# A diffusion backbone step: the feed-forward part's two-operand elementwise work goes from GpSimd to VectorE

## The chip, the cores and the metric

The kernel runs on one core of one Trainium2 chip. The metric is the device time of one execution in microseconds, the median over several runs. The engines are PE (TensorE, matmuls; PEld its weight loads), DVE (VectorE), ACT (ScalarE), POOL (GpSimd) and SP (which issues most DMAs). Each takes its instructions in a fixed order of its own; what waits at the head of an engine's queue holds everything behind it.

## The reference, cut to what matters

Four layers, each a token mixer (of four kinds) and a SwiGLU feed-forward part, over 640 tokens (512 latent and 128 context tokens) of 1024 features:

```python
x = x + m[2] * mixer(modulate(rms_norm(x, norm1_g), m[0], m[1])) @ w_o
h = modulate(rms_norm(x, norm2_g), m[3], m[4])
x = x + m[5] * ((silu(h @ w_gate) * (h @ w_up)) @ w_down)      # 1024 -> 2816 -> 1024
```

Everything is float32. The modulation `m` differs between latent and context tokens.

## The kernel before

**Split products.** PE gets each float32 operand as two tiles, a rounded copy (`whi`, `hh`, `ah`) made by ACT and the remainder (`wlo`, `hl`, `al`) made by a subtraction of two SBUF tiles, and does three matmuls (hi·hi, hi·lo, lo·hi) for each product. `two` (L315 to L320) makes such a pair of a 128x512 weight block; `self.sub` (L608) is the subtraction helper.

**Feed-forward part of a layer** (`rest`, L802 on). It runs in four stages, with the order of instructions on each engine set by a scheduler that follows the priorities in which the code is written.

1. The second half of the mixer's output projection (`halves_first`): 8 feature blocks `d`, each 24 matmuls, then DVE adds the result into `x` (L603), ACT squares (L494, tile `t`), DVE sums the squares (L496). POOL (L621) or ACT (L623) scales `x` by a column for the norm (`scaled`).
2. `make_b` builds the right operands of a one-level Strassen-Winograd product out of the normed activations: DVE multiplies by `rstd` (L656), sums and differences (`T1` to `T4`) follow, and each is split by its inner `two` (hi on ACT at L645 or L648, lo at L608 or L649).
3. Eleven pairs of `gate_up` units (`gate` and `up` for `i` = 0 to 10). A unit loads four 128x512 weight blocks (tiles `raw`), `make_a` forms the sums `S1` to `S4` (L696, tiles `sum`), and seven calls of `block` each split one block and issue 12 matmuls of 128x320 into three PSUM banks `a`, `b`, `d` (tile name `big`). Between them DVE reads the banks (L722, into `sv` or `y`). The accumulation goes on in a bank only when DVE has read it. An `up` unit ends with three products `y*v` (L735), two casts `ah` (L760, ACT) and two subtractions `al` (L608).
4. After pairs 3, 6, 9 and 11 the down projection of the pairs done so far. In the first three layers pieces of the next layer's modulation (`rawm`, `mod`) are filled in.

The four `raw` slots are reused in turn, so the next unit's weight loads wait for the last reader of the old block.

Of the kernel before, what the change touches and what calls it, by code (L numbers as in the profile page):

```python
# [8 lines left out]
F32 = mybir.dt.float32  # L9
F32R = mybir.dt.float32r  # L10
AF = mybir.ActivationFunctionType
ALU = mybir.AluOpType
# [4 lines left out]
ND = 8  # L17
# [19 lines left out]
HALF = ND // 2  # L37
# [225 lines left out]
class Net:  # L263
# [51 lines left out]
    def two(self, raw, eng):  # L315

        hi, lo = (self.slot(n)[:, :raw.shape[1]] for n in ("whi", "wlo"))
        self.nc.scalar.copy(hi, raw)  # L318
        eng.tensor_tensor(lo, raw, hi.bitcast(F32), ALU.subtract)  # L319
        return hi, lo  # L320
# [304 lines left out]
    def make_b(self, pool, L, B, raws):  # L625

        nc = self.nc
        lo, hi = slice(0, 320), slice(320, T)  # L630
        t3 = [pool.tile([P, 2, 320], F32, tag="a", name="raw", bufs=12) for _ in range(HALF // 2)]
        slots = [self.new_act() for _ in range(ND)]
        for tag, w in (("c", T), ("d", 320)):
            slots += [[pool.tile([P, w], F32R, tag=x + tag, name=x, bufs=HALF) for x in ("hh", "hl")] for _ in range(HALF)]
        shift = self.mods[L][0][:, 24:24 + ND]
        more = pool.tile([P, ND + HALF], F32, tag="more", name="more")
        self.sub(nc.gpsimd, more[:, :ND], shift[:, :, 1], shift[:, :, 0])
        self.sub(nc.gpsimd, more[:, ND:], shift[:, HALF:, 0], shift[:, :HALF, 0])

        done = []  # L640

        def two(name, slot, c, x, bias=None, eng=nc.vector):
            h, l = (y[:, c] for y in slots[slot])
            if bias is None:
                nc.scalar.copy(h, x)  # L645
                done.append(self.sub(eng, l, x, h.bitcast(F32)))
            else:
                nc.scalar.activation(h, x, AF.Identity, bias=bias)  # L648
                done.append(eng.scalar_tensor_tensor(l, x, bias, h.bitcast(F32), ALU.add, ALU.subtract))  # L649
            B.setdefault(name, []).append((h, l))  # L650

        def raw(d, c):
            with contextlib.ExitStack() as st:
                if len(done) >= 2:
                    st.enter_context(self.tc.issue_after(done[-2].ins))
                nc.vector.tensor_tensor(raws[d][:, c], raws[d][:, c], self.rstd[:, c], ALU.mult)  # L656

        for d in range(ND):
            raw(d, lo)
            two(("11", "21")[d // HALF], d, lo, raws[d][:, lo], shift[:, d, 0:1])  # L660
            yield
        for i in range(HALF):
            for d in (i, i + HALF):
                raw(d, hi)
                p, m = raws[d][:, NL:], more[:, d:d + 1]
                nc.scalar.activation(p, p, AF.Identity, bias=m)
            a, b, t = raws[i], raws[i + HALF], t3[i // 2][:, i % 2]
            self.sub(nc.vector, t, b[:, hi], a[:, hi])
            self.sub(nc.gpsimd, a[:, hi], a[:, hi], a[:, lo])
            two("T1", i, hi, a[:, hi])  # L670
        for i in range(HALF):
            a, b, t = raws[i], raws[i + HALF], t3[i // 2][:, i % 2]
            nc.vector.tensor_tensor(a[:, lo], t, a[:, lo], ALU.add)
            two("T2", ND + i, lo, a[:, lo], shift[:, i + HALF, 0:1])
            self.sub(nc.gpsimd, b[:, lo], b[:, lo], a[:, lo])
        for i in range(HALF):
            two("T3", ND + i, hi, t3[i // 2][:, i % 2], more[:, ND + i:ND + i + 1])
        for i in range(HALF):
            two("T4", ND + HALF + i, lo, raws[i + HALF][:, lo], eng=nc.gpsimd)
        for i in range(HALF):  # L680
            two("22", i + HALF, hi, raws[i + HALF][:, hi], shift[:, i + HALF, 0:1])
        yield

    def make_a(self, L, name, i):

        nc = self.nc
        at = [WIDX[L, name, f][0] for f in (i, i + NF // 2)]
        raw = {}
        for n in ("21", "22", "11", "12"):
            raw[n] = self.slot("raw")  # L690
            nc.sync.dma_start(raw[n], self.a["wall"][at[int(n[0]) - 1] + int(n[1]) - 1])
        for n, x, y, op in (("S1", "21", "22", ALU.add), ("S2", "S1", "11", ALU.subtract),
                            ("S3", "11", "21", ALU.subtract), ("S4", "12", "S2", ALU.subtract)):
            raw[n] = self.slot("sum")
            eng = nc.vector if n in ("S1", "S2") else nc.gpsimd
            eng.tensor_tensor(raw[n], raw[x], raw[y], op)  # L696
        return raw

    def block(self, out, A, B, start, stop, eng=None):

        h, l = self.two(A, eng or self.nc.vector)
        for k, (xh, xl) in enumerate(B):
            c = slice(k * P, (k + 1) * P)
            self.mm(out, h[:, c], xh, start and k == 0, False)
            self.mm(out, h[:, c], xl, False, False)
            self.mm(out, l[:, c], xh, False, stop and k == len(B) - 1)

    def gate_up(self, fp, L, name, i, B, pair):

        nc = self.nc  # L710
        up = name == "up"
        A = self.make_a(L, name, i)

        eng = nc.vector if i else nc.gpsimd
        a, b, d = (self.ps("big")[:, :320] for _ in range(3))
        t = fp.tile([P, 3, 320], F32, tag="sv", name="sv", bufs=2)
        s1, v1, v2 = (t[:, m] for m in range(3))
        if not up:
            pair.extend(fp.tile([P, T], F32, tag="t", name="y", bufs=4) for _ in range(2))

        def add(out, x, y):
            nc.vector.tensor_tensor(out, x, y, ALU.add)  # L722

        def result(r, c, src, v=None):

            y = pair[r][:, 320 * c:320 * c + 320]
            if not up:
                if v is not None:
                    add(y, src, v)
                self.silu = nc.scalar.activation(y, src if v is None else y, AF.Silu)  # L730
            elif v is None:
                nc.vector.tensor_tensor(y, y, src, ALU.mult)
            else:
                add(v, src, v)
                nc.gpsimd.tensor_tensor(y, y, v, ALU.mult)  # L735

        self.block(a, A["11"], B["11"], True, True, eng)
        yield
        nc.scalar.copy(s1, a)
        self.block(a, A["12"], B["21"], False, True, eng)  # L740
        result(0, 0, a)
        yield
        if i == 0:
            self.block(d, A["S1"], B["T1"], True, True, eng)
        self.block(b, A["S2"], B["T2"], True, True, eng)
        add(v1, b, s1)
        if i:
            self.block(d, A["S1"], B["T1"], True, True, eng)
        self.block(b, A["S3"], B["T3"], False, True)
        yield  # L750
        add(v2, b, s1)
        result(1, 1, d, v2)
        self.block(b, A["22"], B["T4"], False, True)
        result(1, 0, b, s1)
        self.block(d, A["S4"], B["22"], False, True)
        result(0, 1, d, v1)
        if up:
            for r in (1, 0):
                hi, lo = (fp.tile([P, T], F32R, tag="a", name=n, bufs=12) for n in ("ah", "al"))
                nc.scalar.copy(hi, pair[r])  # L760
                self.sub(nc.gpsimd, lo, pair[r], hi.bitcast(F32))
                pair[r] = (hi, lo)
        yield

# [993 lines left out]
```

## Time and profile before

| | |
|---|---|
| median of 3 runs | 3245.66 us (3241.69 to 3249.45) |
| the profiled execution | 3248.49 us, its span 3246.7 us |
| busy in the span | PE 3043.1 us (94%), DVE 2170.4 (67%), ACT 1527.9 (47%), POOL 1257.4 (39%) |
| feed-forward parts | four, some 500 us each |

The span runs from the first to the last instruction. Busy time counts an instruction from its start to its end, waiting for a port included.

### The profile page before, as it was taken

How to read it: one execution, taken by the hardware profiler on the slowest of the kernel's cores; microseconds unless marked ns; L12 is line 12 of the kernel's file. 1: busy time of each engine (PE TensorE's matmuls, PEld its weight loads, DVE VectorE, ACT ScalarE, POOL GpSimd, SP SyncE). 2: the span in 40 equal slices, each digit the busy share in tenths (PEclk: the TensorE clock that was granted, in tenths of full speed). 3: DMA queues.
4: the chain of work that ended last, by engine and by line, in shares of the span. 5: the costliest groups of instructions: out<-in, count | busy, mean ns of one | idle time of the engine just before them, and what ended most of it. 6: DMA issues, size and time to landing. Idle time of an engine off the chain costs nothing. (4 is left out here: it accounts for less than half of the span.)

```text
span 3246.7 us, 58033 instructions
## 1 busy us (share of the span) xinstructions
PE 3043.1 (94%) x21901; PEld 2845.8 (88%) x21901; DVE 2170.4 (67%) x4166; ACT 1527.9 (47%) x3296; POOL 1257.4 (39%) x1175
## 2 busy tenths in 40 slices
PE   8998889999989989999987898999999989799999
PEld 6997879999988779999975677899998878799999
DVE  5555486766576768667668766866765775867665
ACT  4455453433356654334346665433434575534332
POOL 2453362322244454323235445432322553633322
PEclk9998999999999999999998999999999999899999
DMA  7346552233433342222311224422433111122222
GB/s 264 94 122 206 174 196 87 80 106 104 143 104 128 110 153 74 80 82 82 88 46 39 62 74 150 145 77 82 133 106 120 43 37 43 40 85 83 77 85 78
DMA packets 163640, 331.46 MB, mean 102 GB/s; under 512 B 19104, under 2 KB 49184, under 8 KB 163360
## 3 DMA queue, kind: packets, MB, share of 16 engines
q1 hardware_dynamic: 160192, 323.47, 32.3%
q8 instruction: 173, 2.83, 0.4%
q10 hardware_dynamic: 3168, 4.28, 0.4%
q14 instruction: 107, 0.88, 0.1%
HBM read 303.86 MB, written 4.28 MB: 95 GB/s over the span
## 5 line engine op out<-in xcount | busy, mean ns | idle before, releaser
L271 PE MATMUL big<-hh,whi 128*128 128x320 f32 x2720 | 829.5, 314 | 31.3 <-ACT hh L645 12.0
L271 PE MATMUL big<-hl,whi 128*128 128x320 f32 x2720 | 832.9, 312 | 9.6 <-DVE hl L649 5.3
L271 PE MATMUL big<-hh,wlo 128*128 128x320 f32 x2720 | 823.6, 311 | 0.0
L318 ACT CAST whi<-raw 128x512 fp32r<-128x512 f32 (+3 forms) x668 | 388.5, 587 | 655.3 <-PE big L271 407.7
L319 DVE TENSOR_TENSOR wlo<-raw,whi 128x512 fp32r<-128x512 f32 (+1 forms) x504 | 439.2, 874 | 207.0 <-ACT whi L318 204.6
L271 PEld LDWEIGHTS big<-hh,whi 128*128 128x128 f32 x2720 | 509.8, 190 | 47.0 <-DVE sv L722 16.7
L271 PEld LDWEIGHTS big<-hl,whi 128*128 128x128 f32 x2720 | 511.3, 189 | 19.7 <-DVE hl L649 10.6
L271 PEld LDWEIGHTS big<-hh,wlo 128*128 128x128 f32 x2720 | 509.3, 189 | 0.4
L319 DVE TENSOR_TENSOR wlo<-sum,whi 128x512 fp32r<-128x512 f32 x336 | 304.6, 911 | 75.3 <-ACT whi L318 72.5
L319 POOL TENSOR_TENSOR wlo<-raw,whi 128x512 fp32r<-128x512 f32 (+2 forms) x164 | 225.2, 1385 | 305.4 <-ACT whi L318 274.1
L318 ACT CAST whi<-sum 128x512 fp32r<-128x512 f32 x352 | 216.0, 617 | 267.7 <-PE big L271 222.2
L271 PE MATMUL big<-al,whi 128*128 128x320 f32 x1408 | 334.0, 310 | 3.2 <-POOL al L608 3.2
L271 PE MATMUL big<-ah,whi 128*128 128x320 f32 x1408 | 332.0, 311 | 1.2 <-ACT ah L760 1.2
L271 PE MATMUL big<-ah,wlo 128*128 128x320 f32 x1408 | 333.1, 310 | 0.0
L1044 POOL TENSOR_SCALAR p<-p,st 128x640 f32<-128x640 f32 (+2 forms) x256 | 199.4, 784 | 297.0 <-DVE st L1043 188.1
L696 POOL TENSOR_TENSOR sum<-raw 128x512 f32<-128x512 f32 x88 | 124.8, 1418 | 410.3 <-DMA raw<-in_wall 242.3
L735 POOL TENSOR_TENSOR y<-y,sv 128x320 f32<-128x320 f32 x132 | 146.4, 1116 | 346.1 <-DVE sv L722 321.6
L696 POOL TENSOR_TENSOR sum<-raw,sum 128x512 f32<-128x512 f32 x88 | 121.3, 1379 | 404.2 <-ACT whi L318 161.9
L603 DVE SCALAR_TENSOR_TENSOR x<-big,mod,x 128x320 f32<-128x320 f32 (+2 forms) x480 | 182.3, 432 | 107.7 <-PE big L271 107.7
L271 PEld LDWEIGHTS big<-al,whi 128*128 128x128 f32 x1408 | 239.6, 189 | 4.1 <-POOL al L608 3.7
L271 PEld LDWEIGHTS big<-ah,whi 128*128 128x128 f32 x1408 | 238.0, 188 | 4.7 <-issue 2.5
L271 PEld LDWEIGHTS big<-ah,wlo 128*128 128x128 f32 x1408 | 239.3, 189 | 0.2
(264 smaller groups left out, 6093.7 us busy)
## 6 DMA issues: line engine op xcount, KB each, us to landing
raw<-in_wall SPq DMA_DIRECT2D x644, 256.0 KB, 2.6
rawm<-in_wmod SPq DMA_DIRECT2D x176, 512.0 KB, 5.9
k<-k SPq DMA_DIRECT2D x38, 384.0 KB, 4.5
raw<-in_wall SPq DMA_DIRECT2D x96, 128.0 KB, 2.1
bias<-in_nabias SPq DMA_DIRECT2D x16, 576.0 KB, 7.2
raw<-in_wmod SPq DMA_DIRECT2D x32, 256.0 KB, 5.8
qpe<-pes SPq DMA_DIRECT2D x56, 80.0 KB, 2.1
out_y<-x ACTq DMA_DIRECT2D x8, 320.0 KB, 2.2
```

The costliest lines, as they stand in the source:

```text
L271: return self.nc.tensor.matmul(out, lhsT=lhsT, rhs=rhs, start=start, stop=stop, skip_group_check=True)
L318: self.nc.scalar.copy(hi, raw)
L319: eng.tensor_tensor(lo, raw, hi.bitcast(F32), ALU.subtract)
L603: self.last = self.nc.vector.scalar_tensor_tensor(xs, halves[b][:, p0:p1], self.mcol(L, i, d, c), xs, ALU.mult, ALU.add)
L696: eng.tensor_tensor(raw[n], raw[x], raw[y], op)
L735: nc.gpsimd.tensor_tensor(y, y, v, ALU.mult)
L1044: nc.gpsimd.tensor_scalar(p, p, rd, 1.0, ALU.mult, ALU.mult)
```

## The change

Every elementwise instruction with two tensor operands in the feed-forward part that stood on POOL is issued to DVE. In each layer these are 44 sums `S3` and `S4` (128x512), 8 `wlo` of the two units with `i` = 0, 33 products `y*v` (128x320), 22 `al` (128x640), and in `make_b` 12 of 128x320 and two tiny ones: 121 instructions, 484 in all. POOL keeps the scaling at L621, 12 instructions in each layer, and all it does in the mixers.

```diff
@@ make_b
-        self.sub(nc.gpsimd, more[:, :ND], shift[:, :, 1], shift[:, :, 0])
-        self.sub(nc.gpsimd, more[:, ND:], shift[:, HALF:, 0], shift[:, :HALF, 0])
+        self.sub(nc.vector, more[:, :ND], shift[:, :, 1], shift[:, :, 0])
+        self.sub(nc.vector, more[:, ND:], shift[:, HALF:, 0], shift[:, :HALF, 0])
...
-            self.sub(nc.gpsimd, a[:, hi], a[:, hi], a[:, lo])
+            self.sub(nc.vector, a[:, hi], a[:, hi], a[:, lo])
             two("T1", i, hi, a[:, hi])
...
             two("T2", ND + i, lo, a[:, lo], shift[:, i + HALF, 0:1])
-            self.sub(nc.gpsimd, b[:, lo], b[:, lo], a[:, lo])
+            self.sub(nc.vector, b[:, lo], b[:, lo], a[:, lo])
...
-            two("T4", ND + HALF + i, lo, raws[i + HALF][:, lo], eng=nc.gpsimd)
+            two("T4", ND + HALF + i, lo, raws[i + HALF][:, lo])
@@ make_a
             raw[n] = self.slot("sum")
-            eng = nc.vector if n in ("S1", "S2") else nc.gpsimd
-            eng.tensor_tensor(raw[n], raw[x], raw[y], op)
+            nc.vector.tensor_tensor(raw[n], raw[x], raw[y], op)
@@ block and gate_up
-        h, l = self.two(A, eng or self.nc.vector)
+        h, l = self.two(A, self.nc.vector)
...
-        eng = nc.vector if i else nc.gpsimd
...
-                nc.gpsimd.tensor_tensor(y, y, v, ALU.mult)
+                nc.vector.tensor_tensor(y, y, v, ALU.mult)
...
-                self.sub(nc.gpsimd, lo, pair[r], hi.bitcast(F32))
+                self.sub(nc.vector, lo, pair[r], hi.bitcast(F32))
```

The scheduler writes the orders anew. Three places follow. The changed file is three lines shorter, so that L695, L719, L727 and L732 of it are L696, L722, L730 and L735 of before.

The first is DVE in stage 1 of layer 0, from the first sum of the first `gate_up` unit on. Before:

```order
L696 TENSOR_TENSOR sum<-raw 128x512
L603 SCALAR_TENSOR_TENSOR x<-big,mod,x 128x320
L603 SCALAR_TENSOR_TENSOR x<-big,mod,x 128x192
L603 SCALAR_TENSOR_TENSOR x<-big,mod,x 128x128
L696 TENSOR_TENSOR sum<-sum,raw 128x512
L603 SCALAR_TENSOR_TENSOR x<-big,mod,x 128x320
L603 SCALAR_TENSOR_TENSOR x<-big,mod,x 128x192
L603 SCALAR_TENSOR_TENSOR x<-big,mod,x 128x128
L496 TENSOR_TENSOR t<-t 128x640
```

And now:

```order
L695 TENSOR_TENSOR sum<-raw 128x512
L603 SCALAR_TENSOR_TENSOR x<-big,mod,x 128x320
L603 SCALAR_TENSOR_TENSOR x<-big,mod,x 128x192
L603 SCALAR_TENSOR_TENSOR x<-big,mod,x 128x128
L695 TENSOR_TENSOR sum<-raw 128x512
L695 TENSOR_TENSOR sum<-sum,raw 128x512
L319 TENSOR_TENSOR wlo<-raw,whi 128x512
L695 TENSOR_TENSOR sum<-raw,sum 128x512
L603 SCALAR_TENSOR_TENSOR x<-big,mod,x 128x320
L603 SCALAR_TENSOR_TENSOR x<-big,mod,x 128x192
L603 SCALAR_TENSOR_TENSOR x<-big,mod,x 128x128
L319 TENSOR_TENSOR wlo<-raw,whi 128x512
```

`S3`, `S4` and the first `wlo` now stand ahead of the residual additions of `d` = 1; `S4` and the `wlo` need weight blocks that DMAs bring.

The second is ACT in stage 2 of layer 0, around its change of function table; `hh<-raw` at L645 is the first `T1` copy, on which PE waits. Before:

```order
L648 ACTIVATE hh<-raw,more 128x320
L648 ACTIVATE hh<-raw,mod 128x320
L318 CAST whi<-sum 128x512
L730 ACT_TABLE_LOAD
L730 ACTIVATE y<-big 128x320
L645 CAST hh<-raw 128x320
```

And now:

```order
L318 CAST whi<-sum 128x512
L727 ACT_TABLE_LOAD
L727 ACTIVATE y<-big 128x320
L648 ACTIVATE hh<-raw,more 128x320
L648 ACTIVATE hh<-raw,mod 128x320
L318 CAST whi<-raw 128x512
L645 CAST hh<-raw 128x320
```

Two `T` copies and one cast of weights have moved between the table load and the `T1` copy. Layers 1 and 2 show the same; in layer 3 one copy has moved.

The third is DVE at the end of an `up` unit of layer 3; the last `sv` row reads the bank of the unit after it. Before:

```order
L722 TENSOR_TENSOR sv<-big,sv 128x320
L319 TENSOR_TENSOR wlo<-raw,whi 128x512
L722 TENSOR_TENSOR sv<-big,sv 128x320
L319 TENSOR_TENSOR wlo<-sum,whi 128x512 x2
L319 TENSOR_TENSOR wlo<-raw,whi 128x512
L722 TENSOR_TENSOR sv<-big,sv 128x320
```

And now:

```order
L719 TENSOR_TENSOR sv<-big,sv 128x320
L319 TENSOR_TENSOR wlo<-raw,whi 128x512
L695 TENSOR_TENSOR sum<-raw,sum 128x512
L732 TENSOR_TENSOR y<-y,sv 128x320
L719 TENSOR_TENSOR sv<-big,sv 128x320
L319 TENSOR_TENSOR wlo<-sum,whi 128x512
L732 TENSOR_TENSOR y<-y,sv 128x320
L608 TENSOR_TENSOR al<-y,ah 128x640
L319 TENSOR_TENSOR wlo<-sum,whi 128x512
L608 TENSOR_TENSOR al<-y,ah 128x640
L319 TENSOR_TENSOR wlo<-raw,whi 128x512
L719 TENSOR_TENSOR sv<-big,sv 128x320
```

Between the same two reads of PSUM there now stand a sum, two products and two `al` more, and each `al` needs the cast `ah` from ACT. Outside the feed-forward parts the orders are the same but for a few swaps of neighbours in layer 1.

## Rows read from the trace of the kernel before

**Rows 1.** Busy time by engine, the four feed-forward parts together (384:893, 1159:1656, 1975:2482, 2748:3247).

```profile
sum 2012.00, PE 1941.55 PEld 1878.62 DVE 1367.73 ACT 797.77 POOL 724.02; mean PE 485.39 PEld 469.65 DVE 341.93 ACT 199.44 POOL 181.01
```

**Rows 2.** Chain that ended last, layer 3: start us, us, what.

```profile
2873.50 113.62 PE big L271 x773
```

**Rows 3.** Waits of PE, whole span: us in total, times, longest.

```profile
PE big L271 <- ACT hh L645: 12.0, 4, 4.0
PE big L271 <- DVE sv L722: 11.6, 16, 2.1
PE big L271 <- DVE t L496: 10.7, 9, 4.5
...
PE big L271 <- ACT hh L648: 6.7, 8, 1.7
PE big L271 <- DVE hl L649: 5.3, 8, 2.2
...
PE big L271 <- POOL al L608: 3.2, 2, 2.1
```

**Rows 4.** Three groups of DVE by line, whole span: ns min/median/max.

```profile
L319 DVE TENSOR_TENSOR wlo<-sum,whi x336: 672/686/2077, 411.7 to 3197.2; 128x512 fp32r<-128x512 f32 x168
L722 DVE TENSOR_TENSOR sv<-big,sv x308: 472/483/493, 458.3 to 3214.4; 128x320 f32<-128x320 f32 x154
L649 DVE SCALAR_TENSOR_TENSOR hl<-raw,mod,hh x64: 534/540/1424, 422.7 to 2822.9; 128x320 fp32r<-128x320 f32 x64
```

**Rows 5.** Timeline of DVE and POOL at 3192 us: start us, us.

```profile
3192.84 2.08 DVE L319 TENSOR_TENSOR wlo<-sum,whi 128x512 fp32r<-128x512 f32 x1 [0.77 <-ACT whi L318]
...
3192.78 3.57 POOL L608 TENSOR_TENSOR al<-y,ah 128x640 fp32r<-128x640 f32 x2
```

**Rows 6.** Groups by form in 2928:2999 (stage 3, layer 3): busy us, mean ns.

```profile
L319 DVE TENSOR_TENSOR wlo<-raw,whi 128x512 fp32r<-128x512 f32 x17 | 19.8, 1163 | 3.1 <-ACT whi L318 3.0
L319 DVE TENSOR_TENSOR wlo<-sum,whi 128x512 fp32r<-128x512 f32 x21 | 18.9, 899 | 3.9 <-ACT whi L318 3.8
...
L608 POOL TENSOR_TENSOR al<-y,ah 128x640 fp32r<-128x640 f32 x4 | 7.6, 1910 | 0.0
L735 POOL TENSOR_TENSOR y<-y,sv 128x320 f32<-128x320 f32 x6 | 7.4, 1242 | 6.1 <-DVE sv L722 6.1
L696 POOL TENSOR_TENSOR sum<-raw,sum 128x512 f32<-128x512 f32 x5 | 6.5, 1296 | 30.5 <-ACT whi L318 12.5 <-issue 9.1 <-DVE sum L696 8.9
L696 POOL TENSOR_TENSOR sum<-raw 128x512 f32<-128x512 f32 x4 | 5.4, 1346 | 5.3 <-DMA raw<-in_wall 3.0 <-DVE wlo L319 2.3
```

**Rows 7.** Timeline of DVE, stage 1, layer 0.

```profile
398.76 0.82 DVE L496 TENSOR_TENSOR t<-t 128x640 f32<-128x640 f32 x1 [0.81 <-ACT t L494]
399.50 1.13 DVE L603 SCALAR_TENSOR_TENSOR x<-big,mod,x 128x320 f32<-128x320 f32 x3
```

**Rows 8.** Groups by form in 420:457.2 (stage 2, layer 0): busy us, mean ns.

```profile
L649 DVE SCALAR_TENSOR_TENSOR hl<-raw,mod,hh 128x320 fp32r<-128x320 f32 x16 | 11.4, 714 | 0.4 <-ACT hh L648 0.4
L656 DVE TENSOR_TENSOR raw<-raw,rstd 128x320 f32<-128x320 f32 x16 | 10.5, 675 | 0.0
L649 DVE SCALAR_TENSOR_TENSOR hl<-raw,more,hh 128x320 fp32r<-128x320 f32 x4 | 4.7, 1172 | 0.0
...
L608 POOL TENSOR_TENSOR raw<-raw 128x320 f32<-128x320 f32 x8 | 9.6, 1213 | 7.5 <-DVE raw L608 5.9 <-DVE raw L673 1.3 <-DVE mod L439 0.4
L608 POOL TENSOR_TENSOR hl<-raw,hh 128x320 fp32r<-128x320 f32 x4 | 4.0, 1001 | 1.2 <-ACT hh L645 1.2
...
L319 POOL TENSOR_TENSOR wlo<-sum,whi 128x512 fp32r<-128x512 f32 x2 | 2.7, 1343 | 1.6 <-ACT whi L318 1.6
```

**Rows 9.** Timeline of ACT, stage 2, layer 0.

```profile
440.01 0.45 ACT L645 CAST hh<-raw 128x320 fp32r<-128x320 f32 x1
440.36 0.62 ACT L318 CAST whi<-raw 128x512 fp32r<-128x512 f32 x1
440.88 0.56 ACT L648 ACTIVATE hh<-raw,mod 128x320 fp32r<-128x320 f32 x1
```

More of the change, by code (lines that the diff above doesn't have):

```diff
@@ L636, in make_b, with two @@
         more = pool.tile([P, ND + HALF], F32, tag="more", name="more")
-        self.sub(nc.gpsimd, more[:, :ND], shift[:, :, 1], shift[:, :, 0])
-        self.sub(nc.gpsimd, more[:, ND:], shift[:, HALF:, 0], shift[:, :HALF, 0])
+        self.sub(nc.vector, more[:, :ND], shift[:, :, 1], shift[:, :, 0])
+        self.sub(nc.vector, more[:, ND:], shift[:, HALF:, 0], shift[:, :HALF, 0])
         done = []
-        def two(name, slot, c, x, bias=None, eng=nc.vector):
+        def two(name, slot, c, x, bias=None):
             h, l = (y[:, c] for y in slots[slot])
@@ L645, in two @@
                 nc.scalar.copy(h, x)
-                done.append(self.sub(eng, l, x, h.bitcast(F32)))
+                done.append(self.sub(nc.vector, l, x, h.bitcast(F32)))
             else:
                 nc.scalar.activation(h, x, AF.Identity, bias=bias)
-                done.append(eng.scalar_tensor_tensor(l, x, bias, h.bitcast(F32), ALU.add, ALU.subtract))
+                done.append(nc.vector.scalar_tensor_tensor(l, x, bias, h.bitcast(F32), ALU.add, ALU.subtract))
             B.setdefault(name, []).append((h, l))
@@ L694, in make_a, with block @@
             raw[n] = self.slot("sum")
-            eng = nc.vector if n in ("S1", "S2") else nc.gpsimd
-            eng.tensor_tensor(raw[n], raw[x], raw[y], op)
-        return raw
-    def block(self, out, A, B, start, stop, eng=None):
-        h, l = self.two(A, eng or self.nc.vector)
+            nc.vector.tensor_tensor(raw[n], raw[x], raw[y], op)
+        return raw
+    def block(self, out, A, B, start, stop):
+        h, l = self.two(A, self.nc.vector)
         for k, (xh, xl) in enumerate(B):
@@ L734, in result @@
                 add(v, src, v)
-                nc.gpsimd.tensor_tensor(y, y, v, ALU.mult)
-        self.block(a, A["11"], B["11"], True, True, eng)
+                nc.vector.tensor_tensor(y, y, v, ALU.mult)
+        self.block(a, A["11"], B["11"], True, True)
         yield
         nc.scalar.copy(s1, a)
-        self.block(a, A["12"], B["21"], False, True, eng)
+        self.block(a, A["12"], B["21"], False, True)
         result(0, 0, a)
@@ L743, in gate_up @@
         if i == 0:
-            self.block(d, A["S1"], B["T1"], True, True, eng)
-        self.block(b, A["S2"], B["T2"], True, True, eng)
+            self.block(d, A["S1"], B["T1"], True, True)
+        self.block(b, A["S2"], B["T2"], True, True)
         add(v1, b, s1)
         if i:
-            self.block(d, A["S1"], B["T1"], True, True, eng)
+            self.block(d, A["S1"], B["T1"], True, True)
         self.block(b, A["S3"], B["T3"], False, True)
```

## The prediction

> **What bounds the kernel now.** I read the busy time by engine in the feed-forward parts first, since the change is only there. PE works in 1941.55 of 2012 us [rows 1]: 70 us of idle time in four parts is all that the change can give back. Then the chain that ended last: for stretches of a hundred microseconds it is nothing but matmuls, 773 of them in 113.62 us, 0.147 us each [rows 2]. In stage 3 PE is the bound, and DVE matters only where PE waits for it. So the third view is the list of PE's waits [rows 3]. The ones that belong to the feed-forward part and that the change can reach are the first `T1` copy (L645, 12.0 us in 4 waits, one in each layer), the reads of PSUM by DVE (L722, 11.6 us in 16), the sum of squares (L496, 10.7 us in 9), the other copies and remainders of `make_b` (L648 6.7 us, L649 5.3 us), and `al` on POOL (3.2 us in 2, at the very end of a part). The fourth view is how long DVE's instructions take. The 336 `wlo` of a sum have a median of 686 ns and a longest of 2077, while the 308 reads of PSUM, of which one operand lies in SBUF, stay within 472 to 493 [rows 4]. The timeline shows what the long ones have in common: the 2.08 us `wlo` lies beside two `al` on POOL, 3.57 us together [rows 5]. DVE instructions with two operands in SBUF are held up while POOL works on SBUF too.
>
> **The change, part by part: DVE's load.** On DVE a 128x640 instruction takes 0.82 us and the next one starts 0.74 us after it [rows 7]: 0.08 us of each overlaps. A moved 128x512 then costs 0.60 us of DVE's queue (0.686 less 0.08), a 128x320 0.40 (from 0.48), an `al` 0.74.
>
> In 71 us of stage 3 [rows 6] POOL has 4 `al`, 6 products and 9 sums; on DVE they are 4 x 0.74 + 6 x 0.40 + 9 x 0.60 = 10.8 us. Against that the 17 and 21 `wlo` have means of 1163 and 899 ns where 686 is the undisturbed median: 17 x 0.477 + 21 x 0.213 = 12.6 us that end when POOL is silent. DVE's load falls by 1.8 us in place of rising. The other stretches of stage 3 repeat the pattern.
>
> The 12.6 us can be held against a rule. The Trainium skill, SBUF — State Buffer, section "SBUF: two separate sides", says that DVE with two SBUF inputs and a GpSimd instruction that reads SBUF exclude each other: whichever starts first has the shared ports for its whole length, and the other is blocked. By that rule alone up to all of POOL's work in the stretch could be put on DVE's account, and the load would fall by more; the measured means decide, and they say 12.6.
>
> In stage 2 of layer 0 [rows 8] DVE has a stretch of 37 us from the first `rstd` product to the last remainder with no idle time to speak of. Of it 16 x (0.714 - 0.540) + 16 x (0.675 - 0.48) + 4 x (1.172 - 0.540) = 8.4 us are such waits (the undisturbed times are in [rows 4]), and smaller groups of the same kind add some 3. What moves in are 8 + 4 instructions of 128x320 (4.8 us), two `wlo`, and three sums that the same view lists (5 x 0.60 = 3.0). Net 8.4 + 3 - 7.8: DVE gets through stage 2 about 4 us sooner, at least 0.6 if the small groups give nothing.
>
> **What reaches PE.** Term by term, over the four layers:
>
> - `al` at the end of a part [rows 3]: 1.9 us on POOL [rows 6] becomes 0.82 on DVE, twice in a row, and the product ahead of it 0.48 for 1.24. The wait of 3.2 us goes: -3. The bounds are -3.2 and 0, if the DVE queue holds something else by then.
> - Remainders in stage 2 (L649, 5.3 us): DVE is 4 us sooner at the end of a stretch in which these waits are 1 or 2 us long. I take -4 (bounds -5.3 and 0).
> - The `T1` copy: ACT now does two copies and a cast ahead of it [rows 9]. Start to start the cast is 0.52 us and a copy of 0.56 about 0.46, so the copy comes 1.45 us later in three layers and 0.46 in the fourth: +4.8, and PE stands still there already, so nothing hides it. The bounds are +4.8 and 0, if ACT gets to its table load sooner.
> - Copies at L648 (6.7 us in 8): some of the waits come right behind the `T1` one, for exactly the copies that now stand ahead of it. -3 (bounds -6.7 and 0).
> - Reads of PSUM (L722, 11.6 us in 16): DVE is late for them when a held-up instruction of up to 2.08 us is in front. The longest in front is now 0.82, but there are more of them. -3, bounds -9 and what the second rival says.
> - Stage 1 (L496, 10.7 us): sums and `wlo` now stand ahead of the residual additions, ten instructions or 6 us in some 25 us, where DVE has idle time like the 0.81 us in front of its row [rows 7]. Moving the `raw` blocks' readers to DVE frees the slots sooner, too, while S4 waiting for its DMA holds the additions. I take 0, bounds -6 and +6.
> - The two tiny subtractions, and `wlo` of the first units, are in the loads above; weight DMAs are issued by SP as before, and the slots come free at about the same time.
>
> The sum is -3 - 4 + 4.8 - 3 - 3 + 0 = -8.2 us against the profiled execution's 3248.49, so 3240.3. The median of the runs shown is 2.8 us under that execution; for a median I say 3237.
>
> **The rivals.**
>
> *Hidden.* PE bounds the kernel, and each microsecond won in stage 2 is lost at the `T1` copy or in stage 1. For it: the gains in the list are no larger than the doubtful terms. Against it: three of the five waits have their cause removed. Time: the terms -3 and -4 against +4.8, with the rest at zero, -2: 3243.
>
> *DVE in front of PSUM (slower).* In a `gate_up` unit the bank `b` goes on accumulating only when DVE has read it, and what covers that read is one block of 12 matmuls, 12 x 0.147 = 1.76 us [rows 2]. At the end of an `up` unit a sum, two products and two `al` now stand between two reads, 0.60 + 0.80 + 1.48 = 2.9 us of work, and an `al` waits for a cast on ACT. If the read comes 1 us later than its cover in each of the 44 `up` units, it costs 44 us: 3290. It decides as soon as the mean delay beyond the cover exceeds 8.2/44 = 0.19 us. Against it: in the 71 us of [rows 6] DVE's load does not rise, and over the whole span PE waited for these reads 16 times only [rows 3]. By the Trainium skill, Perfetto Trace Analysis, section "Optimizing Scalar/DVE Operations", a saturated DVE is a reason to put work on Scalar or even GPSIMD, which speaks against this change; the same section warns that between those two it might not help, as they share a read port. DVE at 1367.73 of 2012 us [rows 1], waits included, isn't saturated over a part, but it is in stage 2.
>
> *More comes back.* If stage 1 gives its 6 us and the reads their 9 as well, with -3, -5 and -6 from the others and the `T1` copy no later: about -29, so 3217.
>
> *The change doesn't do what it says.* The 48 scalings stay on POOL and go on colliding with DVE in stage 1. That leaves stage 1 as it is, which the 0 for it already says.
>
> **How the numbers follow.** The forecast of about -8 has a chance of 0.50 and by itself runs from -16 to -4; hidden 0.27; slower 0.16; more 0.07. The range of 3221 to 3256 reaches from most of the large gain to a mean delay beyond the cover of (3256 - 3237)/44 = 0.43 us in front of PSUM, and leaves out the rest of both, under 0.2. A difference of 0.2%, 6.5 us, is about what a measurement of this kernel can tell from none. Of the forecast 0.43 lies beyond it, and all of the large gain: faster 0.50. Hidden and the small end of the forecast are the same: 0.33. Slower 0.17.
>
> **What would show it.** Right: `wlo` of a sum with a longest time under 1 us in stage 3; DVE's busy time over the span within 2% of before though it has 484 instructions more; PE's wait for `al` gone, for L649 under 2 us; its wait for L645 up to some 16 us. Wrong: PE's waits for the reads of PSUM grown to 20 us and more (the second rival), waits for L496 or for the residual additions grown (stage 1), or DVE busy far above 2170 us, which would say that the long `wlo` had another cause than POOL.

## The result, and the profile after

The changed kernel takes 3219.73 us (median of 4 runs, 3214.83 to 3222.39) against 3247.55 us before (4 runs): a ratio of 0.9913, 95% interval 0.9891 to 0.9935. That is 27.8 us less, where 8.2 were forecast. The direction is right, the size is a third of what came, and 3219.73 lies just under the range (3221 to 3256); the rival *more comes back* had said 3217.

The forecast of DVE's load held. In the feed-forward parts (windows view; busy us by engine, the four parts summed) DVE is busy 1397.67 us for 1367.73 [rows 1], though 484 instructions more stand on it:

```profile
sum 1984.70, PE 1924.07 PEld 1870.83 DVE 1397.67 ACT 804.62 POOL 82.75; mean PE 481.02 PEld 467.71 DVE 349.42 ACT 201.15 POOL 20.69
```

In the 71 us of stage 3 of [rows 6], DVE was busy 56.91 us with 83 instructions. The same place of the changed kernel (windows view: stretch, then busy us and instructions of PE, PEld, DVE, ACT and POOL, granted clock):

```profile
2907.00:2978.00 71.00, 71.00 (x486) 71.00 (x485) 54.08 (x101) 32.67 (x61) 0.00 (x0) 1.00 0.28 84
```

101 instructions in 54.08 us: DVE does more and is busy for less, since the long instructions are gone. The three groups of [rows 4], after (ns min/median/max):

```profile
L319 DVE TENSOR_TENSOR wlo<-sum,whi x352: 673/684/694, 397.0 to 3164.8; 128x512 fp32r<-128x512 f32 x176
L719 DVE TENSOR_TENSOR sv<-big,sv x308: 475/484/493, 448.0 to 3183.6; 128x320 f32<-128x320 f32 x154
L649 DVE SCALAR_TENSOR_TENSOR hl<-raw,mod,hh x64: 533/543/554, 415.6 to 2795.7; 128x320 fp32r<-128x320 f32 x64
```

The longest `wlo` of a sum falls from 2077 to 694 ns, the longest `hl` from 1424 to 554; the reads of PSUM were never long and are the same.

PE's waits over the span, after (us in total, times, longest; they answer to [rows 3]):

```profile
PE sm L271 <- DMA rawm<-in_wmod: 30.0, 13, 4.8
...
PE big L271 <- DVE t L496: 8.3, 6, 3.5
...
PE big L271 <- ACT hh L645: 5.2, 2, 4.4
...
PE big L271 <- DVE hl L649: 3.4, 8, 1.1
...
PE big L271 <- DVE sv L719: 2.2, 2, 1.6
...
PE big L271 <- ACT hh L648: 1.7, 2, 1.2
...
PE big L271 <- DVE al L608: 0.3, 1, 0.3
```

Every wait that the prediction priced got smaller, and one that it didn't name got larger. The same view of before had, for the modulation's blocks:

```profile
PE sm L271 <- DMA rawm<-in_wmod: 9.0, 5, 2.4
```

So the sum of the list says less than it seems to. A better account is PE's *lost time*, worked out from the records of all matmuls: from each start to the next, less the pace of its form at full clock (0.147 us for 128x320; 2.05 us is set for the 32 matmuls of a modulation piece, where an undisturbed one in stage 3 adds 1.96, so the account is 0.1 us too low for each piece, before and after alike). A low granted clock is in it, the useful work of a piece is not. An entry is good to some 1 us where a piece stands at the border of two columns. In us, layers 0 to 3:

| | stage 1 | stage 2 and the first two units | the rest of the part | sum |
|---|---|---|---|---|
| before | 5.1, 3.6, 3.5, 11.1 | 12.9, 16.3, 13.2, 20.9 | 8.2, 11.9, 7.6, 6.0 | 120.3 |
| after | 5.9, 3.3, 3.3, 9.4 | 13.5, 14.4, 17.8, 15.8 | 3.8, 5.4, 3.8, -0.7 | 95.7 |

The feed-forward parts give back 24.6 us, and 21.4 of these lie behind the first two units: in stage 3, where PE waited for the reads of PSUM, and at the ends of the parts. Counted from start to start, the reads alone are 12.1 us of it (13 of the 16 waits of before lie there, and none after), `al` and `ah` some 4, and a low granted clock some 3. Stage 2 gives 5.1 us in layer 3, and in layers 0 to 2 it loses 3.3. The profiled executions differ by 33.7 us (3248.49 to 3214.83); what is left lies in the mixers, where orders hardly changed. PE starts stage 1 of layer 0 at 384.5 us before and 375.7 after; in the runs below, whose first mixer has the same code, it starts between 376.4 and 385.2. So some 9 us between two single profiles can be chance, and times are compared by medians.

Where PE waited for a read. Before, in the last `up` unit ahead of the first down projection of layer 0 (timeline of DVE, then of POOL: start us, us):

```profile
505.33 2.07 DVE L319 TENSOR_TENSOR wlo<-sum,whi 128x512 fp32r<-128x512 f32 x1 [0.77 <-ACT whi L318]
507.32 2.05 DVE L319 TENSOR_TENSOR wlo<-raw,whi 128x512 fp32r<-128x512 f32 x1
509.29 0.48 DVE L722 TENSOR_TENSOR sv<-big,sv 128x320 f32<-128x320 f32 x1
...
502.68 2.63 POOL L735 TENSOR_TENSOR y<-y,sv 128x320 f32<-128x320 f32 x2
505.27 3.55 POOL L608 TENSOR_TENSOR al<-y,ah 128x640 fp32r<-128x640 f32 x2
```

Both `wlo` ahead of the read at 509.29 lie beside the two `al` on POOL: 3.96 us from the start of the first to the read. After, at the same place, both `al` are on DVE as well:

```profile
496.57 0.81 DVE L608 TENSOR_TENSOR al<-y,ah 128x640 fp32r<-128x640 f32 x1
497.31 0.68 DVE L319 TENSOR_TENSOR wlo<-sum,whi 128x512 fp32r<-128x512 f32 x1
497.91 0.81 DVE L608 TENSOR_TENSOR al<-y,ah 128x640 fp32r<-128x640 f32 x1
498.65 0.68 DVE L319 TENSOR_TENSOR wlo<-raw,whi 128x512 fp32r<-128x512 f32 x1
499.25 0.48 DVE L719 TENSOR_TENSOR sv<-big,sv 128x320 f32<-128x320 f32 x1
```

Four instructions in 2.68 us where two took 3.96. Such a wait, 0.2 to 1.3 us long, stood ahead of 10 of the 12 down projections that end the first three groups of pairs; after, there is none.

### The profile page after: what moved, and what is told of

It reads as the page before. It is cut to its first block, busy times and chain, and to the rows that moved or that the text cites. A ratio compares the mean times of both kernels' runs of the same rounds, so it can differ in the third digit from the quotient of the medians.

```text
span 3213.0 us, 57617 instructions
## 1 busy us (share of the span) xinstructions
PE 3027.1 (94%) x21901; PEld 2839.4 (88%) x21901; DVE 2199.0 (68%) x4650; ACT 1534.5 (48%) x3296; POOL 606.8 (19%) x691
## 5 line engine op out<-in xcount | busy, mean ns | idle before, releaser
L271 PEld LDWEIGHTS big<-hl,whi 128*128 128x128 f32 x2720 | 510.0, 189 | 11.9 <-DVE hl L649 6.5
L319 POOL TENSOR_TENSOR wlo<-raw,whi 128x512 fp32r<-128x512 f32 (+2 forms) x148 | 197.0, 1343 | 1638.2 <-ACT whi L318 1600.5
L319 DVE TENSOR_TENSOR wlo<-raw,whi 128x512 fp32r<-128x512 f32 (+1 forms) x520 | 329.6, 638 | 119.2 <-ACT whi L318 116.0
L271 PE MATMUL big<-al,whi 128*128 128x320 f32 x1408 | 327.4, 309 | 0.3 <-DVE al L608 0.3
L271 PE MATMUL big<-ah,whi 128*128 128x320 f32 x1408 | 325.4, 310 | 0.4 <-ACT ah L757 0.3
L319 DVE TENSOR_TENSOR wlo<-sum,whi 128x512 fp32r<-128x512 f32 x352 | 241.0, 685 | 60.2 <-ACT whi L318 57.8
L271 PE MATMUL sm<-whi,hh 128*128 128x256 f32 (+1 forms) x770 | 224.2, 296 | 2.1 <-DVE qs L287 1.2
L271 PE MATMUL sm<-wlo,hh 128*128 128x256 f32 (+1 forms) x770 | 222.6, 291 | 0.2 <-POOL wlo L319 0.2
L271 PE MATMUL sm<-whi,hl 128*128 128x256 f32 (+1 forms) x770 | 222.7, 291 | 0.0
```

The lines of the kernel that those rows point to most:

```text
L271: return self.nc.tensor.matmul(out, lhsT=lhsT, rhs=rhs, start=start, stop=stop, skip_group_check=True)
```

## The experiments

The times are medians, and each ratio is to runs of the kernel before that were taken beside that run. The lost times are of one profiled execution each. Five runs move a part of the change, and tail_back moves the rest of it:

| moved to DVE | label | us | ratio to before (95%) | PE's lost time: stage 1, 2, rest |
|---|---|---|---|---|
| all (the change) | | 3219.73 | 0.9913 (0.9891 to 0.9935) | 21.9, 61.5, 12.3 |
| products and `al` | tail_only | 3217.23 | 0.9915 (0.9902 to 0.9928) | 25.2, 60.4, 13.4 |
| `al` | al_only | 3228.83 | 0.9947 (0.9930 to 0.9964) | 25.7, 65.6, 17.6 |
| products | products_only | 3247.21 | 0.9997 (0.9986 to 1.0008) | 27.0, 61.6, 35.5 |
| sums `S3`, `S4` | sums_only | 3244.30 | 0.9995 (0.9986 to 1.0004) | 34.4, 60.6, 20.6 |
| `make_b`, first `wlo` | stage2_only | 3248.86 | 1.0009 (1.0000 to 1.0018) | 19.3, 55.9, 36.3 |
| all but products and `al` | tail_back | 3229.72 | 0.9951 (0.9939 to 0.9964) | 25.6, 58.3, 19.3 |
| nothing | before | 3246.31 to 3248.55 | | 23.3, 63.3, 33.7 |

**tail_only.** Against before:

```diff
-                nc.gpsimd.tensor_tensor(y, y, v, ALU.mult)
+                nc.vector.tensor_tensor(y, y, v, ALU.mult)
...
-                self.sub(nc.gpsimd, lo, pair[r], hi.bitcast(F32))
+                self.sub(nc.vector, lo, pair[r], hi.bitcast(F32))
```

> Only the products y*v and the al remainders go to DVE; the sums S3 and S4, the first wlo and all of make_b stay on POOL. Theory A (POOL's products and al lengthen the DVE instructions that stand in front of a read of PSUM, and PE then waits for that read): PE's wait for sv falls from 11.6 us to about 3, the wait for al from 3.2 to under 0.5, and the time is 12 to 15 us under before, about 3234. Rival B (DVE's load: the sums still collide, and DVE has 55 instructions of a layer more): the waits for sv stay at 10 or grow, and the time is within 5 us of before.

55 of a layer's 121 instructions give the whole gain; the run cannot be told from the full change. The waits for `sv` fall from 11.6 us to

```profile
PE big L271 <- DVE sv L720: 2.6, 5, 0.8
```

Theory A's waits hold (no wait for `al` is left), its time does not: it expected 12 to 15 us, and 29 came. Rival B falls: the sums go on colliding, and tail_only is no slower than the full change for it.

**sums_only.** Against before:

```diff
-            eng = nc.vector if n in ("S1", "S2") else nc.gpsimd
-            eng.tensor_tensor(raw[n], raw[x], raw[y], op)
+            nc.vector.tensor_tensor(raw[n], raw[x], raw[y], op)
```

> Only the sums S3 and S4 go to DVE. Theory A: the waits for sv in front of the down projections stay (8 to 12 us), since the products and al still run on POOL at that place, and so do the waits for al; the time is 0 to 5 us under before. Rival C (the sums are what matters, as they are the most instructions and also free the weight slots sooner): sv under 4 us and the time 12 us under before or more.

No change in time, as theory A said, but not for its reason. In the profiled execution, the slowest of its 11, the sums do relieve stage 3 (33.7 to 20.6 us lost), and give it back in stage 1 (23.3 to 34.4): the sums that now stand ahead of the residual additions there hold up the sum of squares. About half of these 11 us are longer waits; with them the granted clock was at its lower level, 1.2 GHz, for 24 us of stage 1 in place of 3.

```profile
PE big L271 <- DVE t L496: 16.8, 7, 5.4
...
PE big L271 <- DVE sv L720: 6.3, 5, 3.0
```

**stage2_only.** Against before, the edits in `make_b` and in `block` of the change alone:

```diff
-            self.sub(nc.gpsimd, a[:, hi], a[:, hi], a[:, lo])
+            self.sub(nc.vector, a[:, hi], a[:, hi], a[:, lo])
...
-        h, l = self.two(A, eng or self.nc.vector)
+        h, l = self.two(A, self.nc.vector)
```

> Only the work of make_b and the wlo of the first two units go to DVE. Theory A: stage 2 of layers 0 to 2 gains nothing, since PE then waits for the modulation's weight blocks (rawm) in place of the T1 copy, and layer 3, which has no such pieces, gains about 5 us; the time is 4 to 6 us under before. Rival D (the 20 us of rawm waits are chance of one execution): all four layers gain 3 to 5 us each, 15 us in all.

No gain by the median. Layer 3 loses 15.4 us in stage 2 for 20.9, as in the full change, and layers 0 to 2 40.5 for 42.4. The profiled execution was the fastest of 12 (3234.11 us) and its feed-forward parts lose 8.8 us less than before, so profile and median do not agree here; what made the others slower is not known.

**tail_back.** Against the changed kernel:

```diff
-                nc.vector.tensor_tensor(y, y, v, ALU.mult)
+                nc.gpsimd.tensor_tensor(y, y, v, ALU.mult)
...
-                self.sub(nc.vector, lo, pair[r], hi.bitcast(F32))
+                self.sub(nc.gpsimd, lo, pair[r], hi.bitcast(F32))
```

> The changed kernel, with the products y*v and the al remainders back on POOL. Theory A: the waits for sv and al return with some 8 and 3 us and the time is 10 to 15 us over the changed kernel, about 3232. Rival C or D (sums or stage 2 carry the gain): within 4 us of the changed kernel, about 3221.

The time is as theory A said, 10 us over the change, and one half of its reason is wrong: `al` comes back as a wait, `sv` does not.

```profile
PE big L271 <- POOL al L608: 3.2, 2, 2.1
...
PE big L271 <- DVE sv L719: 2.2, 2, 1.5
```

With the sums off POOL its queue is short; at the place shown above the products and the first `al` start earlier, and only one `al` is left beside the `wlo` ahead of the read. So either half of the change takes away most of the waits for reads, and their gains don't add up. What only the tail gives is the ends of the parts (the rest falls from 19.3 to 12.3 us, most of the 10 us).

**al_only and products_only.** Against before, the second or the first line of tail_only's diff alone.

> Of the whole change only the 22 al remainders of a layer go to DVE; sums, products, the first wlo and make_b stay on POOL. Theory G (the two al of an up unit, 3.6 us in a row on POOL, are what lengthens the two wlo in front of the next read of PSUM, and what PE waits for at the end of a part): the time is that of the run with products and al, 3216 to 3224, with waits for sv under 4 us. Rival H (each set of collisions adds its part, and the products are half of them): half the gain, about 3232, with 5 to 8 us for sv.

> Of the whole change only the 33 products of a layer go to DVE; al, sums, the first wlo and make_b stay on POOL. Theory G (al is the main cause): al on POOL goes on lengthening the wlo in front of the reads, so sv stays at 6 to 10 us and al at 3; the time is 5 to 12 us under before, about 3238. Rival N (the products, which hold up POOL's queue and with it the casts and al behind them, are the main cause): sv under 3 us, 15 us under before or more.

`al` alone gives 18 us, between the two theories, with 6.9 us left for `sv` in 7 waits. None of the 7 stands ahead of a down projection any more: all lie in stage 2 or within 11 us behind the first two units, so theory G is right on that place and not on the whole. Products alone give nothing, where theory G expected 5 to 12 us (`sv` 14.7 us in 20), but with `al` already on DVE they give another 10 to 12. Which waits these are worth is not shown: the lost time falls by 5 us in stage 2 and by 4 behind it.

**al_decoy.** Is it the collision, or the shorter way from `ah` to PE? Against al_only, one instruction more, whose result nobody reads:

```diff
                 self.sub(nc.vector, lo, pair[r], hi.bitcast(F32))
+                self.sub(nc.gpsimd, fp.tile([P, T], F32, tag="junk", name="junk"), pair[r], hi.bitcast(F32))
```

> As the run with al alone on DVE, and beside it POOL subtracts the same two SBUF tiles once more into a tile that nobody reads; the orders on PE and DVE stay the same but for a few swaps. No result waits for POOL's copy. Theory A (the collision on SBUF makes DVE late): the wlo beside it reach 2 us again, the waits for sv come back with 6 to 10 us, and the time is 8 to 15 us over the run with al alone. Rival I (latency: PE and ACT gained since an al takes 0.82 us on DVE and 1.8 on POOL, and the place of al in the order is what counts): no wait comes back, and the time is within 3 us of the run with al alone.

3289.90 us against 3228.83: 61 us longer, ratio to before 1.0135 (1.0115 to 1.0156), four times the upper end of what theory A expected. At one place of al_only (DVE), where a sum on POOL lies beside the first `wlo` and nothing beside the rest:

```profile
594.16 1.78 DVE L319 TENSOR_TENSOR wlo<-sum,whi 128x512 fp32r<-128x512 f32 x1
595.87 0.81 DVE L608 TENSOR_TENSOR al<-y,ah 128x640 fp32r<-128x640 f32 x1
596.60 0.68 DVE L319 TENSOR_TENSOR wlo<-raw,whi 128x512 fp32r<-128x512 f32 x1
597.21 0.48 DVE L720 TENSOR_TENSOR sv<-big,sv 128x320 f32<-128x320 f32 x1
```

The same four in al_decoy (DVE, then POOL):

```profile
597.27 1.79 DVE L319 TENSOR_TENSOR wlo<-sum,whi 128x512 fp32r<-128x512 f32 x1
598.98 2.19 DVE L608 TENSOR_TENSOR al<-y,ah 128x640 fp32r<-128x640 f32 x1
601.09 2.03 DVE L319 TENSOR_TENSOR wlo<-raw,whi 128x512 fp32r<-128x512 f32 x1
603.04 0.48 DVE L720 TENSOR_TENSOR sv<-big,sv 128x320 f32<-128x320 f32 x1
...
598.46 4.11 POOL L608 TENSOR_TENSOR junk<-y,ah 128x640 f32<-128x640 f32 x2
```

From the first `wlo` to the read it takes 5.77 us in place of 3.05, and PE stands 1.84 us at that read. Over the span:

```profile
PE big L271 <- DVE sv L720: 46.8, 31, 3.6
```

These waits grew by 39.9 us. Most of what is left of the 61 us is the clock: behind the first two units al_only has none of the lower level, al_decoy 41 us of it in eleven stretches, each begun at the end of one of these waits or right behind it, which is up to 20.5 us lost. At the place shown, ahead of the wait of 1.84 us and behind it (windows view; the clock is the third number from the end):

```profile
590.00:600.00 10.00, 10.00 (x71) 10.00 (x70) 9.42 (x11) 4.65 (x9) 7.24 (x5) 1.00 0.29 80
604.00:607.00 3.00, 3.00 (x14) 3.00 (x14) 1.29 (x4) 1.59 (x3) 0.00 (x0) 0.56 0.30 87
```

It is the mechanism of the second rival, brought about by POOL and not by DVE's own load; that 46.8 us is near the rival's price of 44 is chance, since it fell on 31 reads and not on 44. Rival I, latency, is out: nothing waits for POOL's copy, and DVE's instructions keep their order but for 3 of 4254. The copy could also hold up the products and sums behind it in POOL's queue. The records of the 31 reads speak against that: since DVE's last read of PSUM (6 us back at most) its instructions took 89.6 us more than undisturbed ones, and it stood idle for 7.6 us.

**rawm_early, fewer_pieces, late_after, late_before: where stage 2's gain went.** rawm_early, against the changed kernel, gives `rawm` two tiles more and loads one piece ahead:

```diff
+        more = 2 if pool.name.startswith('ffn') else 0
...
-... tag="rawm", name="rawm", bufs=BURST))
+... tag="rawm", name="rawm", bufs=BURST + more))
...
         self.mod_load(pool)
+        if pool.name.startswith('ffn'):
+            self.mod_load(pool)
```

> The changed kernel with six rawm tiles for four, so that half of the next modulation piece is loaded while PE waits for or works on the present one. Theory J (in stage 2 of layers 0 to 2 PE now waits for rawm, 30.0 us in 13, and that has eaten what DVE gained there): the rawm waits fall to under 15 us and the time is 6 to 12 us under the changed kernel, about 3210. Rival K (the T1 copy is as late, and the piece only stands in front of it): the waits go back to the T1 copy (L645 from 5 to 12 us), and the time is within 4 us of the changed kernel.

3218.55 us, 0.9915 (0.9895 to 0.9935): not told from the change. The waits for `rawm` fall from 30.0 to

```profile
PE sm L271 <- DMA rawm<-in_wmod: 13.1, 9, 2.7
```

and stage 2 of layers 0 to 2 loses 37.9 us for 45.7, but that profile is the fastest of its 6 runs, and more of the pieces stand in stage 2 there (15 for 10). It leans to theory J without settling it.

fewer_pieces takes the two early calls of `fill` away (the last two lines of the diff) and raises the count of the later ones by two (`1 - EDGE`); late_after and late_before take them away too, leave the count as it is, and create the filler only behind stage 2 (of the changed kernel and of before):

```diff
             if L + 1 < self.depth:
-                self.filler = [self.mod_parts(L + 1, c0, 6144, fp)]
...
             next(B_steps)
+            if L + 1 < self.depth:
+                self.filler = [self.mod_parts(L + 1, c0, 6144, fp)]
...
-            self.fill(EDGE)
             done = 0
```

> The changed kernel, with the two modulation pieces that are issued right behind stage 1 left to stage 3 (the count of the later ones is raised by two). Theory J: the rawm waits fall by 10 us or more, and the time by 5 us or more. Rival K: PE waits for the T1 copy and for make_b instead, and the time is the same or up to 5 us longer, since two pieces of 1.9 us that filled the wait now stand elsewhere.

> The changed kernel, with the modulation pieces of layers 0 to 2 begun only behind stage 2, so that stage 2 of these layers has none, as in layer 3. Theory L (the pieces in stage 2 and their late blocks took what DVE gained there): stage 2 of layers 0 to 2 loses some 5 us each, as layer 3 did, the rawm waits in stage 2 end, and the time is 10 to 16 us under the changed kernel, about 3206. Rival M (the pieces fill time in which PE would stand for the T1 copy): the waits go to L645 (from 5 to 15 us) and the time is within 4 us of the changed kernel or up to 6 us over it.

> The same shift of the modulation pieces in the kernel before. Theory L: make_b with its collisions sets stage 2 there, as in layer 3 (20.9 us of PE's lost time with no pieces, 19.6 in the others), so the time stays within 4 us of before. Rival M: the time rises by 4 to 10 us, as PE has nothing to do while it waits.

fewer_pieces: 3220.04 us. late_after: 3240.25 us, 20 over the change; late_before: 3265.38, 17 over before. None of the three tests what it was made for. The scheduler put the pieces back: in late_after seven of layer 0's twelve run by 475 us, as in the change (seven by 472 us), and since the count was not raised, two calls more are left to the end, and the last pieces run past the end of the part. The next mixer waits for these: from the end of layer 0's part to stage 1 of layer 1 it takes 278.2 us, for 263.1 in the change.

**held_after, held_before, held_tail.** Here the filler again begins behind stage 2, and a piece is queued on PE behind a matmul of a later unit. So all pieces stand in stage 3, and the count is raised by four, so that none is left to the end of the part:

```diff
-                    while done < todo * (m + 1) // len(mats):
-                        self.fill(1)
+                    while m > 3 and done < todo * (m - 2) // (len(mats) - 4):
+                        with tc.issue_after(self.held.ins):
+                            self.fill(1)
```

> The changed kernel, with every modulation piece of the feed-forward part queued on PE behind a matmul of a later unit, so that all of them stand in stage 3. Theory L (late modulation blocks took the gain in stage 2): PE's lost time in stage 2 of layers 0 to 2 falls from 20.8, 18.1 and 25.1 us to some 16 each, as in layer 3, and the time is 10 to 16 us under the changed kernel, about 3206. Rival M (the pieces fill waits that are there anyway): 12 us of waits return at L645 and L648, and the time is within 4 us of the changed kernel or above it.

> The same hold in the kernel before. Theory L: with its collisions stage 2 loses some 20 us in layer 3 without a piece, so layers 0 to 2 stay at some 19 to 20 us, and the time is within 4 us of before. Rival M: above it by 4 us or more.

> Products and al on DVE, the rest on POOL as before, and the pieces held in stage 3. Theory L: make_b collides with POOL as before, so the hold gives nothing: within 4 us of the run with products and al, 3217. Rival M: some us above it.

The lost times in these expectations, and in late_before's, still counted most of a piece's own matmuls as lost: 20.8, 18.1 and 25.1 there are 13.5, 14.4 and 17.8 in the account of this document, under layer 3 and not over it. Theory L owed much of its look to that.

| pieces held in stage 3 | us | over the same kernel without the hold | lost in stage 2, layers 0 to 3 |
|---|---|---|---|
| the change (held_after) | 3236.19 | 16.5 | 16.2, 15.8, 15.8, 15.8 |
| products and `al` (held_tail) | 3259.98 | 42.8 | 19.8, 19.8, 20.7, 20.1 |
| before (held_before) | 3299.20 | 51.5 | 19.7, 20.2, 20.8, 20.2 |

Theory L gave the right number for stage 2 and the wrong time; rival M is right. Without pieces stage 2 loses 20 us in every layer with `make_b` on POOL and 15.8 with it on DVE: the gain is there, 4.4 us in each layer. But the pieces do fill waits. They brought the 20 down to 14 (42.4 in three layers) before the change, and the 15.8 only to 15.2 after it, since they now wait for their blocks themselves. Of held_after's waits:

```profile
PE big L271 <- ACT hh L645: 17.5, 4, 4.4
...
PE sm L271 <- DMA rawm<-in_wmod: 1.8, 1, 1.8
```

The time that the hold costs is not all in stage 2. It also takes away the two pieces that stood in stage 1 of layers 0 to 2, and stage 1 of the change then loses 37.3 us for 21.9 (10.7, 8.1 and 8.3 in these layers for 5.9, 3.3 and 3.3): nearly all of held_after's 16.5 us. Its stage 2 loses 2.1 us more. For held_tail it is 11 us more in stage 1 and 20 in stage 2, for held_before 20 and 18, and 12 behind them. So the pieces in stage 2 were worth some 18 to 20 us with `make_b` on POOL and 2 with it on DVE.

And moving the sums, the first `wlo` and `make_b` to DVE, which is worth nothing between tail_only and the change (3217.23 and 3219.73), is worth 23.8 us between held_tail and held_after (3259.98 and 3236.19). Of their two profiles the lost time differs by 17 us, all in stage 2 (80.4 to 63.6).

## Why the prediction went wrong, step by step

- **DVE's load: right.** It said that DVE would do 484 instructions more in about the same busy time; 2170.4 us became 2199.0 over the span, and in the 71 us of stage 3 DVE's time fell by 2.8 us where 1.8 were forecast. What one collision costs can be read in al_decoy: the two instructions ahead of the read last 4.22 us in place of 1.49 (0.81 and 0.68), so 2.7 us are lost. POOL's two copies beside them take 4.11 us. The shortest of the 88 copies takes 1.56 us, so two are some 3.1 us of work, and POOL lost the other 1.0 us itself. The Trainium skill, SBUF — State Buffer, section "SBUF: two separate sides", says that of a DVE instruction with two SBUF inputs and a GpSimd instruction that reads SBUF, whichever starts first has the shared ports for its whole length, and the other is blocked. The trace agrees with it but for 0.4 us at this place: 2.7 us of POOL's 3.1 are lost to DVE.
- **Reads of PSUM: -3 forecast, -9.4 came** (11.6 to 2.2 us; 12.1 behind the first two units alone, counted from start to start). This is the term that failed: the mechanism was right, its size a third of the true one. The prediction saw that a long instruction in front makes DVE late, and took only a quarter of the wait off, because there would be more instructions in front. It didn't look at one of the waits. The timeline at 505 us shows both `wlo` ahead of the read beside both `al`; taking these off POOL shortens that stretch even with the `al` on DVE, 3.96 to 2.68 us. What came lies just past the lower bound of -9, which was put down as a bound and not as the forecast. With `al` the forecast for what lies behind the first two units was -6, and -21.4 came.
- **Ends of the parts: -3 forecast for `al`, -2.9 came** (3.2 to 0.3 us), and two things beside it. `ah` waits less (1.2 to 0.3 us), since the product ahead of it is sooner; and the granted clock keeps its upper level. Around these waits in layer 1 the windows view gave, before (PE had stood for 0.6 and 2.1 us):

```profile
1625.00:1640.00 15.00, 12.88 (x78) 12.61 (x77) 6.58 (x15) 3.49 (x5) 3.93 (x4) 0.89 0.11 29
```

  and after:

```profile
1604.00:1619.00 15.00, 14.73 (x100) 14.47 (x100) 9.41 (x21) 4.24 (x6) 1.09 (x1) 1.00 0.11 29
```

  A mean of 0.89 is a share of the stretch at 1.2 in place of 2.4 GHz: 0.11 x 15 = 1.7 us lost on top of the wait, and the same in layer 3 (0.89 and 1.00). The sum had no such term; it was put at nothing without a reason.
- **The `T1` copy: +4.8 forecast, and the wait fell, 12.0 to 5.2 us.** This step was wrong as it was worked out. It counted two copies and a cast as new in front of the `T1` copy. ACT before, layer 0:

```profile
435.36 0.56 ACT L648 ACTIVATE hh<-raw,more 128x320 fp32r<-128x320 f32 x1
435.83 0.55 ACT L648 ACTIVATE hh<-raw,mod 128x320 fp32r<-128x320 f32 x1
437.75 0.62 ACT L318 CAST whi<-sum 128x512 fp32r<-128x512 f32 x1 [1.37 <-PE big L271]
438.39 1.28 ACT L730 ACT_TABLE_LOAD   x1
439.68 0.44 ACT L730 ACTIVATE y<-big 128x320 f32<-128x320 f32 x1
440.01 0.45 ACT L645 CAST hh<-raw 128x320 fp32r<-128x320 f32 x1
```

  and after:

```profile
427.67 0.62 ACT L318 CAST whi<-sum 128x512 fp32r<-128x512 f32 x1 [1.31 <-PE big L271]
428.31 1.28 ACT L727 ACT_TABLE_LOAD   x1
...
429.94 0.55 ACT L648 ACTIVATE hh<-raw,more 128x320 fp32r<-128x320 f32 x1
430.39 0.55 ACT L648 ACTIVATE hh<-raw,mod 128x320 fp32r<-128x320 f32 x1
430.84 0.60 ACT L318 CAST whi<-raw 128x512 fp32r<-128x512 f32 x1
431.35 0.46 ACT L645 CAST hh<-raw 128x320 fp32r<-128x320 f32 x1
```

  The two copies stood ahead of the `T1` copy before as well, only ahead of the table load; one cast is new. Counted from the first matmul of the first unit, the copy starts at 17.2, 18.1, 15.2 and 16.6 us before and at 16.3, 18.3, 15.3 and 14.5 after. The wait is smaller where PE has a modulation piece in front of it, which then waits for DMA (the waits for `rawm` grew by 21 us). Where none stands in front, it did grow, by less than forecast: in layer 3 from 3.99 to 4.38 us, and in held_after it is 4.38 us in each of the four layers, for 3.4 to 4.0 in held_before.
- **Stage 2: -4 and -3 forecast for L649 and L648.** The list says -1.9 and -5.0, near enough (L649 is left with 3.4 us, where a right forecast was to show under 2), but the lost time of stage 2 fell by 1.8 us only, all of it from layer 3. That the three terms of stage 2 add up to -2.2 is luck: none of them came as priced, and the waits moved to `rawm`. DVE did get through sooner; the modulation pieces had already been using that time, as the held runs show. This is the rival *hidden*, true for stage 2 and for no other stage.
- **Stage 1: 0 forecast, -1.4 came.** The sums alone cost 11 us there. That stage 2's group alone gives 4 is weakly shown, since the other kernels that leave the sums on POOL differ by as much among themselves (23.3 to 27.0 us in stage 1). So of the two effects that the prediction set against each other one is shown.
- **The second rival** did not come in the change, and its mechanism is real: al_decoy shows it with 46.8 us. **The fourth** said that the 48 scalings left on POOL go on colliding: they do so in part. No `wlo` of a sum is over 694 ns, but beside a scaling three sums of the changed kernel took 1.10 us where the median of the 88 is 0.69.

So `al` and the products behind the last reads of an `up` unit are enough for the whole gain, 55 of the 121 instructions. The other 66 give 17 us when they go alone (tail_back), and nothing on top. The best version measured is tail_only by its median, and no run tells it from the full change.

## What to carry to other kernels

Here work moved off POOL was worth what DVE's next time-critical instruction won, not what either engine's load won: open the timeline at one of the waits, and see what runs on POOL beside the instructions ahead of it. Two causes of one wait don't add up, and a gain in a stretch where a filler already uses the idle time is no gain: look at what PE does in the wait before pricing its end. In two orders side by side, count as added only what was not ahead of the instruction in the old one, on either side of a table load.

## What the runs showed of the hardware that was not expected

One idle subtraction on POOL for each `al` (88 in all) cost 61 us, 0.7 us each, although nobody waited for its result; about a third of it is the granted clock, which went to 1.2 GHz behind eleven of the waits. And POOL's instructions are not all alike to DVE: two-operand ones lengthened `wlo` to 2.08 us, while beside the scaling by a column (L621) 27 `wlo` of the changed kernel, counted from its records, stayed at or under 693 ns. Three of these lie wholly inside a scaling of 1.57 us, the time that one takes alone, so neither was held up; where a `wlo` started together with a scaling, the scaling took 2.11 us. It is no rule for all of DVE's instructions, as the three sums of 1.10 us show, and what decides it is not shown.
